# Gaps between on-chip tiles, and two pools swapped, in a one-core hybrid encoder layer

## The chip, the core and the metric

The kernel runs on one core of a Trainium2 chip, as one program. The metric is the device time of one execution in microseconds (us). The core has a matrix engine (TensorE, PE in the profile, whose weight loads have a row of their own, PEld), three engines for elementwise work (VectorE or DVE, ScalarE or ACT, GpSimd or POOL), and a queue on SyncE (SP) that issues most DMAs. Tiles lie in on-chip memory of 128 partitions; a tile's address is a byte offset that is the same in every partition.

## The reference, cut to what matters

```python
proj = x @ w_in                                  # 2048 tokens, 1024 -> 1312 columns
q  = rms(c_q) @ w_q_b;  kv = rms(c_kv) @ w_kv_b  # 8 heads, 64 + 32 rotary, values 64
o_mla = softmax(q @ k.T * 96**-0.5) @ v          # dense, 8 heads, all 2048 keys
o_swa = banded_softmax(q_s, k_s, sinks) @ v_s    # |t - s| <= 128, 8 heads, 2 key heads
x = layer_norm(alpha * x + concat(o_mla, o_swa) @ w_o)
h = conv3(x @ w_up) + conv_b;  g, u = split(h)   # 2 x 2816 columns
x = layer_norm(alpha * x + (gelu(g) * u) @ w_down)
```

## The kernel before

Every product is made of float32 values that are split into a high and a low part, both in the matrix engine's float32r type. `PASSES = ((0, 0), (0, 1), (1, 0))` are the three matmuls that one step of a product takes: high by high, high by low, low by high. A matmul names two on-chip operands: `lhsT`, the weights (128 columns, 512 bytes of each partition), and `rhs`, which is streamed (at most 512 columns, 2,048 bytes of each partition). Each matmul is preceded by its own weight load.

The five stages follow each other, and in each the matmuls stand in an order written out by hand:

1. **Projection and window attention** (lines 494 to 880). Per 128 tokens: three column groups of `w_in` (L598: weights `xT`, streamed `wi`; 16 tiles x 24 matmuls of 512 columns for each of two groups, and of 288 columns for the third), the low-rank products (L372: weights `cT`, streamed `wq` in 384 columns and `wkv` in 512; 192 each), window scores (L754: weights `q2`, streamed `kT`, 256 matmuls, 224 of them with 384 columns) and window values (L798: weights `vS`, streamed `pT`, 184 matmuls).
2. **Dense attention** (`Mla`, 8 heads x 16 query blocks, 128 periods). Per period 12 score matmuls (L205: weights `qT`, 96 rows, streamed `kT`), 16 transposes of the probabilities (L157: the data as weights, `ident` streamed, 128 columns), 8 value matmuls (L175: weights `v2`, streamed `pt`).
3. **Output projection** (`out_proj`, 16 tiles x 48 matmuls, L981: weights `mh`, for the first tile `m0`; streamed `wo`), layer norm, transposes and the sums that a Strassen-like scheme of 7 products takes, stored to `yS`.
4. **Up-projection** (`up_products`, 3,696 matmuls, L1382). Weights: five buffers `u0` to `u4`, used in turn, 12 matmuls each. Streamed: the 14 operand tiles `y00` to `y61` in pools `y_a` and `y_b`.
5. **Down-projection** (`down_products`, L1402). Seven stretches i = 0 to 6 of 264 matmuls. Weights: `a0`, `a1`. Streamed: in the odd stretches tiles `B` of pool `d_b`; in the even ones eleven tiles in places that the stage before has left: `r00` to `r11` and `T0`, `u0` to `u2`, and `T1`, `u3`, `u4`.

Pools are stacks: the left ones grow up from the constants, the right ones grow down from byte 229,344. A tile is rounded up to 32 bytes, and nothing else is aligned. 229,344 is 480 past a multiple of 512, and the right-hand tiles that are operands are whole multiples of 512 bytes, so they lie 480 past such a multiple. On the left the offset depends on the small tiles that stand below.

A tile may take a place that an earlier tile had; its first writer then waits for the last reader of the earlier one. One such place matters here. In `ffn`, pool `y_b` takes the place of `out_proj`'s pools: tile `y30` (101,152 to 109,344) has the place of `g1` and `b1`, the norm's gain and bias. It is written by `split_op(0, 3)` (L1098 and L1099) in step t = 0 of `up_products`; in step 1 follows, on the same ScalarE queue, the copy `s1` of the first product (L1246), which the third product (L1382, X) waits for. `b1` is read last by the POOL addition of the last tile's norm (L919). `y[ts]` is stored at L1017 on SP's queue, and on the same queue the next operand pieces are loaded (L1089) when `split_op` has read the ones before.

Of the kernel before, what the change touches and what calls it, by code (L numbers as in the profile page):

```python
# [12 lines left out]
F32 = mybir.dt.float32  # L13
# [8 lines left out]
P = 128  # L22
# [320 lines left out]
class Kern:  # L343
# [23 lines left out]
    def mm3(self, out, n, lhs, rhs):  # L367

        nc = self.nc
        for k in range(n):  # L370
            for i, (l, r) in enumerate(PASSES):
                nc.tensor.matmul(out, lhsT=lhs(k, l), rhs=rhs(k, r),  # L372
                                 start=(k == 0 and i == 0), stop=(k == n - 1 and i == 2))

    def consts(self, pool):
        nc = self.nc
        self.ident = pool.tile([P, P], F32, name="ident")
        make_identity(nc, self.ident)
        self.cw = pool.tile([P, 4, 2 * NF], F32, name="cw")
        one = pool.tile([P, 1], F32, name="one")  # L380
        nc.gpsimd.memset(one, 1.0)
        nc.scalar.copy(one, one)
        self.mhalf = pool.tile([P, 1], F32, name="mhalf")
        nc.gpsimd.memset(self.mhalf, -0.5)

    def warm_up(self, ps):

        t = ps.tile([P, 512], F32, name="M")
        for i in range(16):
            self.nc.tensor.transpose(out=t[:, i % 4 * P:(i % 4 + 1) * P], in_=self.ident, identity=self.ident)  # L390
# [103 lines left out]
    def project(self, mla, keep, heads_pool):  # L494
        nc, tc, a = self.nc, self.tc, self.a
        wide = ExitStack()
        with ExitStack() as st:
            pool = self.pools(st)
            wip = self.pools(wide)("p1wi", 1, side="right")
            cst = pool("p1c", 1)  # L500
# [10 lines left out]
            wsrc = w_in.rearrange("(k p) c -> p k c", p=P)  # L511
            wq = [cst.tile([P, 2, H * DQ], F32R, name=f"wq{i}") for i in range(2)]
            wkv = [cst.tile([P, 2, H * 128], F32R, name=f"wkv{i}") for i in range(2)]
            gcol = cst.tile([P, 4], F32, name="gcol")
            sink = cst.tile([P, SH], F32, name="sink")
            sink8 = cst.tile([P, SH], F32, name="sink8")
# [28 lines left out]
            sm = pool("p1s", 2)  # L545
# [36 lines left out]

            kT = [cst.tile([P, SKV, 6, P], F32R, name=f"kT{i}") for i in range(2)]
            nc.gpsimd.memset(kT[1].bitcast(F32), 0.0)

            qTs, vSs = {}, {}
# [82 lines left out]
            def latents_t(n):  # L671
                cn = cns.pop(n)
                t = psT.tile([P, 512], F32, name="T")
                for j in range(4):
                    nc.tensor.transpose(out=t[:, j * P:(j + 1) * P], in_=cn[:, j * P:(j + 1) * P], identity=self.ident)
                cT = cTs[n] = [sm.tile([P, 4, P], F32R, name=f"cT{i}", bufs=1) for i in range(2)]
                o = [v.rearrange("p k t -> p (k t)") for v in cT]
                nc.scalar.copy(o[0], t)
                nc.vector.tensor_sub(o[1], t, o[0].bitcast(F32))
# [61 lines left out]
            def window_p(n, g, d):  # L741

                lo, hi = span(n)
                assert hi - 1 in vSs
                nb = hi - lo
                nk = nb * P
                q2 = qTs[n]
                sl = slice(lo % 4, lo % 4 + nb)
                s = st8[n, g] = big.tile([P, 4, 384], F32, name="s", bufs=2)
                mx = sm.tile([P, 4], F32, name="mx")  # L750
                for j in range(4):
                    sp = psS.tile([P, 512], F32, name="Sp")
                    for i in range(2):
                        nc.tensor.matmul(sp[:, 0:nk], lhsT=q2[:, g * 4 + j], rhs=kT[i][:, g, sl], start=(i == 0), stop=(i == 1))  # L754
                    slope = 2.0 ** (-(g * 4 + j + 1))
                    nc.vector.scalar_tensor_tensor(s[:, j, 0:nk], d, -8.0 * slope, sp[:, 0:nk], op0=ALU.mult, op1=ALU.add)
                    if j % 2:
                        nc.vector.reduce_max(mx[:, j - 1:j + 1], s[:, j - 1:j + 1, 0:nk], axis=AX.X)
                    if j == 1:
                        yield  # L760
                hs = slice(g * 4, g * 4 + 4)
                nm = sm.tile([P, 4], F32, name="nm")
                nc.vector.tensor_max(nm, mx, sink8[:, hs])
                nc.vector.tensor_scalar(nm, nm, -0.125, 1.0, op0=ALU.mult, op1=ALU.mult)
                es = sm.tile([P, 4], F32, name="es")
                nc.vector.tensor_add(es, sink[:, hs], nm)
                sums = sm.tile([P, 4], F32, name="sums")
                for j in range(4):
                    nc.scalar.activation(s[:, j, 0:nk], s[:, j, 0:nk], AF.Exp, bias=nm[:, j:j + 1], scale=0.125,
                                         accum_out=sums[:, j:j + 1])  # L770
                nc.scalar.activation(es, es, AF.Exp)
                nc.vector.tensor_add(sums, sums, es)
                rec = sm.tile([P, 4], F32, name="rec")
                nc.vector.reciprocal(rec, sums)
                for j in range(4):
                    nc.gpsimd.tensor_scalar(s[:, j, 0:nk], s[:, j, 0:nk], rec[:, j:j + 1], 1.0, op0=ALU.mult, op1=ALU.mult)
# [41 lines left out]
            def do(token, n):  # L818
# [6 lines left out]
                elif name in ("x0", "x1"):  # L825
                    if m + 2 < NT and (name, m) not in gens:
                        gens[name, m] = x_parts(m + 2, int(name[1]))
                elif m < 0 or m >= NT:
                    return
                elif name in ("fk", "fq", "lt", "ds"):  # L830
                    if (name, m) not in gens:
                        gens[name, m] = {"fk": front_k, "fq": front_q, "lt": latents_t, "ds": distances}[name](m)
                elif name in ("k0", "k1", "k2", "k3"):
                    c = int(name[1])
                    mla.prep_k(0, c, psT)
                    mla.prep_v(0, c)
                    if c < 2:
                        mla.load_kv(0, c + 2)
                elif name == "q0":
                    mla.prep_q(0, 0, psT)  # L840
                elif name == "cl":
                    wide.close()
                    mla.open_heads(keep, heads_pool)
                    for c in range(2):
                        mla.load_kv(0, c)
                        mla.load_q(0, c)
                else:
                    if (name, m) not in gens:
                        gens[name, m] = (window_p(m, int(name[1]), gens["ds", m]) if name[0] == "p" else
                                         {"la": latents, "sq": swa_q, "sk": swa_kv, "hd": heads, "wo": window_o}[name](m))  # L850
                    if next(gens[name, m], gens) is gens:
                        done.add((name, m))
# [85 lines left out]
    def out_proj(self):  # L938
        nc, tc, a, wo = self.nc, self.tc, self.a, self.wo
        with ExitStack() as stack:  # L940
# [2 lines left out]
            self.op = [self.pools(self.opsA)("y_a", 1)]  # L943
            self.ops = [None] * 7
            pool = self.pools(stack)
            cst = pool("o_c", 1)
            sm = pool("o_s", 3)
            mp = pool("o_m", 2)
            yp = pool("o_y", 1)
            psT = pool("oT", 4, space=PSUM)  # L950
            psM = pool("oM", 4, space=PSUM)
# [113 lines left out]
    def open_weights(self):  # L1065

        w = self.wst = self.top("w_st", 1)
        self.FS = [f for i in range(NP) for f in (i, i + NP)] * 2
        self.prods = {7 * n + o: (n, s) for n in range(2 * NF) for s, o in enumerate(self.OFF)}
        self.rank = {t: i for i, t in enumerate(sorted(self.prods))}  # L1070
        self.r = [[w.tile([P, 2, 512], F32, name=f"r{q}{m}") for m in range(2)] for q in range(2)]
        self.u = [w.tile([P, 2, 512], F32R, name=f"u{i}") for i in range(3)]
        self.Tt = [w.tile([P, 2, 512], F32, name="T0")]
        self.hb = w.tile([P, 2, NF], F32, name="hb")

    def more_weights(self, pool):
        self.up = pool
        self.u += [pool.tile([P, 2, 512], F32R, name=f"u{i}") for i in range(3, self.UNITS)]
        self.Tt += [pool.tile([P, 2, 512], F32, name="T1"), pool.tile([P, 512], F32, name="T2")]
# [507 lines left out]
```

## Time and profile before

| | |
|---|---|
| median of 3 runs | 2936.74 us (2935.35 to 2937.01) |
| the profiled execution's own time | 2936.55 us |
| its span, first to last instruction | 2934.8 us |
| TensorE busy | 97% of the span, 13,943 matmuls |
| VectorE, ScalarE, GpSimd busy | 72%, 52%, 35% |
| mean granted TensorE clock | 0.988 of 2.4 GHz |

A matmul's shown duration includes a pipeline that the next matmul overlaps. The pace of matmuls is therefore read from the timeline, which merges neighbours of one kind into a row: the start of the next row less the start of this one, by the count of this one. A row of matmuls that follows a row of transposes also carries the end of the last transpose.

### The profile page before, as it was taken

How to read it: one execution, taken by the hardware profiler on the slowest of the kernel's cores; microseconds unless marked ns; L12 is line 12 of the kernel's file. 1: busy time of each engine (PE TensorE's matmuls, PEld its weight loads, DVE VectorE, ACT ScalarE, POOL GpSimd, SP SyncE). 2: the span in 40 equal slices, each digit the busy share in tenths (PEclk: the TensorE clock that was granted, in tenths of full speed). 3: DMA queues.
4: the chain of work that ended last, by engine and by line, in shares of the span. 5: the costliest groups of instructions: out<-in, count | busy, mean ns of one | idle time of the engine just before them, and what ended most of it. 6: DMA issues, size and time to landing. Idle time of an engine off the chain costs nothing.

```text
span 2934.8 us, 39778 instructions
## 1 busy us (share of the span) xinstructions
PE 2845.6 (97%) x13943; PEld 2345.6 (80%) x13943; DVE 2123.5 (72%) x3393; ACT 1527.5 (52%) x2830; POOL 1038.5 (35%) x1349
## 2 busy tenths in 40 slices
PE   8999998899999999999998999999999998999997
PEld 7888886688888888887787888887888887888875
DVE  6666676677777777777666888889877777666576
ACT  5555554667767776776233544445544444332332
POOL 4334343588888888887323000000000000000112
PEclk9999999899999999999999999999999999999999
DMA  4222222111101110111776645557545445955453
GB/s 155 82 71 81 72 58 68 37 33 33 31 24 33 33 31 24 33 31 48 215 241 216 190 147 152 158 161 231 153 140 148 142 138 189 340 198 178 159 178 114
DMA packets 353565, 349.95 MB, mean 119 GB/s; under 512 B 35184, under 2 KB 284372, under 8 KB 353364
## 3 DMA queue, kind: packets, MB, share of 16 engines
q1 hardware_dynamic: 350396, 337.80, 37.1%
q10 hardware_dynamic: 2968, 9.60, 1.0%
q8 instruction: 110, 1.80, 0.2%
q14 instruction: 91, 0.75, 0.1%
HBM read 223.06 MB, written 120.08 MB: 117 GB/s over the span
## 4 chain that ended last, share of the span: by engine, by line
PE 81%; DVE 7%; POOL 4%; DMA 3%; issue 3%; ACT 3%; SPq 0%; POOLq 0%; DVEq 0%; ACTq 0%
PE X L1382 12%; PE Sp L205 12%; PE D L1402 11%; PE W L1382 8%; PE O L175 8%; PE T L157 8%; PE M L598 5%; PE Y L1382 4%; PE Z L1382 4%; PE M L981 3%; DMA pw<-prow 2%; PE M L372 2%; PE M L798 1%; PE Sp L754 1%; PE T L787 1%
## 5 line engine op out<-in xcount | busy, mean ns | idle before, releaser
L205 PE MATMUL Sp<-kT,qT 96*128 96x512 f32 x1536 | 388.3, 402 | 5.9 <-ACT p L215 3.1
L1382 PE MATMUL X<-y,u 128*128 128x512 f32 x1584 | 385.1, 396 | 7.9 <-ACT s L1246 7.9
L207 DVE TENSOR_REDUCE mx<-Sp 128x1 f32<-128x1024 f32 x256 | 313.1, 1224 | 90.2 <-PE Sp L205 76.0
L1382 PEld LDWEIGHTS X<-y,u 128*128 128x128 f32 x1584 | 299.3, 189 | 78.2 <-ACT s L1246 8.3
L243 POOL TENSOR_SCALAR p<-p,rec 128x1024 f32<-128x1024 f32 x255 | 284.4, 1126 | 141.2 <-ACT stg L111 89.7
L205 PEld LDWEIGHTS Sp<-kT,qT 96*128 96x128 f32 x1536 | 281.0, 190 | 62.5 <-ACT p L215 4.9
L1455 POOL TENSOR_TENSOR patch<-hb 128x11 f32<-128x11 f32 x4 | 2.9, 735 | 874.6 <-ACT hb L1267 874.6
L215 ACT ACTIVATE p<-Sp,nm 128x1024 f32<-128x1024 f32 x256 | 287.7, 1124 | 5.4 <-DVE nm L209 5.3
L157 PE MATMUL T<-ident,p 128*128 128x128 f32 x2048 | 278.0, 276 | 5.8 <-POOL p L243 2.3
L157 PEld LDWEIGHTS T<-ident,p 128*128 128x128 f32 x2048 | 236.8, 141 | 56.4 <-POOL p L243 23.2
L224 ACT CAST pt<-T 128x512 fp32r<-128x512 f32 x256 | 137.8, 589 | 258.2 <-PE T L157 258.2
L598 PE MATMUL M<-wi,xT 128*128 128x512 f32 (+1 forms) x1152 | 267.4, 368 | 4.0 <-ACT wi L519 2.5
L175 PE MATMUL O<-pt,v 128*128 128x512 f32 x1024 | 271.2, 407 | 0.0
L1382 PE MATMUL W<-y,u 128*128 128x512 f32 x1056 | 259.6, 395 | 2.8 <-DVE hr L1287 2.8
L1382 PEld LDWEIGHTS W<-y,u 128*128 128x128 f32 x1056 | 198.4, 188 | 50.1 <-ACT hr L1251 2.1
L598 PEld LDWEIGHTS M<-wi,xT 128*128 128x128 f32 x1152 | 200.5, 190 | 36.0 <-ACT wi L519 2.9
L175 PEld LDWEIGHTS O<-pt,v 128*128 128x128 f32 x1024 | 183.4, 189 | 35.7 <-DVE pt L228 0.9
L1402 PE MATMUL D<-B,a 128*128 128x512 f32 x792 | 183.8, 394 | 4.9 <-DVE a L1443 4.9
L1402 PEld LDWEIGHTS D<-B,a 128*128 128x128 f32 x792 | 150.5, 190 | 37.7 <-DVE a L1443 6.1
L113 POOL TENSOR_TENSOR pt<-stg,pt 128x512 fp32r<-128x512 f32 x128 | 165.7, 1295 | 10.7
L228 DVE TENSOR_TENSOR pt<-T,pt 128x512 fp32r<-128x512 f32 x256 | 163.9, 681 | 2.7 <-ACT pt L224 2.5
L355 POOL TENSOR_TENSOR n2y<-n2ve,mhalf 128x1 f32<-128x1 f32 x16 | 26.6, 1663 | 393.2 <-DVE n2ve L1485 388.2
(317 smaller groups left out, 5553.5 us busy)
## 6 DMA issues: line engine op xcount, KB each, us to landing
r<-in_w_up SPq DMA_DIRECT2D x154, 256.0 KB, 3.6
araw<-hS SPq DMA_DIRECT2D x55, 704.0 KB, 4.2
oy<-in_w_down SPq DMA_DIRECT2D x132, 256.0 KB, 4.7
hS<-gs SPq DMA_DIRECT2D x110, 256.0 KB, 2.4
tS<-T SPq DMA_DIRECT2D x88, 256.0 KB, 2.2
T<-tS SPq DMA_DIRECT2D x88, 256.0 KB, 2.9
qkv<-nat SPq DMA_DIRECT2D x32, 512.0 KB, 5.4
oy<-yS SPq DMA_DIRECT2D x28, 512.0 KB, 5.8
```

The source lines that it names most:

```text
L113: nc.gpsimd.tensor_tensor(dst[1], sv, dst[0].bitcast(F32), op=ALU.subtract)
L157: nc.tensor.transpose(out=t[:, i * P:(i + 1) * P], in_=p[g // 2][:, k0:k0 + P], identity=self.k.ident)
L175: nc.tensor.matmul(ov, lhsT=vb, rhs=pt[w][:, i], start=(g == 0 and i == 0 and w == 0), stop=(g == 3 and i == 3 and w == 1))
L205: nc.tensor.matmul(sp[:, cc * 512:(cc + 1) * 512], lhsT=q[l], rhs=self.kTs[h][r][:, k0:k0 + 512], start=(i == 0), stop=(i == 2))
L207: nc.vector.reduce_max(mx[:, hf:hf + 1], sp, axis=AX.X)
L215: nc.scalar.activation(p[hf], sps[hf], AF.Exp, bias=nm, scale=self.scale, accum_out=sums[:, hf:hf + 1])
L224: nc.scalar.copy(o[g][0], self.k4(ts[g]))
L228: nc.vector.tensor_sub(o[g][1], self.k4(ts[g]), o[g][0].bitcast(F32))
L243: eng.tensor_scalar(p[hf], p[hf], rec, 1.0, op0=ALU.mult, op1=ALU.mult)
L598: nc.tensor.matmul(ov, lhsT=h[l][:, k % 4], rhs=wi[g][r][:, k], start=(k == 0 and i == 0), stop=(k == KD - 1 and i == 2))
L1382: nc.tensor.matmul(bk[n, bank], lhsT=w[:, l, k * P:(k + 1) * P], rhs=o[r][:, k], start=bool(new) and k == 0 and i == 0, stop=k == KH - 1 a ...
L1402: self.nc.tensor.matmul(d, lhsT=a[l][:, k], rhs=self.Bs[i, k][:, r], start=(k == 0 and x == 0), stop=(k == NP - 1 and x == 2))
```

## The change

Eight tiles are allocated that nothing reads or writes ("gaps"), and in `out_proj` the pool `o_m` (the tiles `mh`) is opened ahead of the pools `o_c` (`g1`, `b1`) and `o_s` (small tiles of the norm). No instruction is added, removed or reordered.

```diff
+    @staticmethod
+    def gap(pool, n, name="gap"):
+        pool.tile([P, n // 4], F32, name=name, bufs=1)
...
         nc.gpsimd.memset(self.mhalf, -0.5)
+        self.gap(pool, 96)
...
             wkv = [cst.tile([P, 2, H * 128], F32R, name=f"wkv{i}") for i in range(2)]
+            self.gap(cst, 384, "gap2")
...
+            self.gap(cst, 32)
             kT = [cst.tile([P, SKV, 6, P], F32R, name=f"kT{i}") for i in range(2)]
+            self.gap(cst, 384, "gap3")
...
+                if n == 0:
+                    self.gap(sm, 192)
                 cT = cTs[n] = [sm.tile([P, 4, P], F32R, name=f"cT{i}", bufs=1) for i in range(2)]
...
+                if n == 0 and g == 0:
+                    self.gap(sm, 448, "gap2")
                 rec = sm.tile([P, 4], F32, name="rec")
...
+            mp = pool("o_m", 2)
             cst = pool("o_c", 1)
             sm = pool("o_s", 3)
-            mp = pool("o_m", 2)
...
         self.hb = w.tile([P, 2, NF], F32, name="hb")
+        self.gap(w, 96)
```

What it does to the places, worked out from the tiles' order and sizes (bytes past a multiple of 512; w is the weights' operand, s the streamed one):

| matmuls | before | after |
|---|---|---|
| L598 | w 96, s 480 | w 480, s 480 |
| L372 | w 416, s 384 | w 480, s 480 |
| L754 | w 96, s 480 | w 480, s 480 |
| L798 | w 416, s 480 | w 480, s 480 |
| L205 | w 480, s 480 | the same |
| L175 | w 480, s 384 | w 480, s 480 |
| L981, tiles 1 to 15 | w 448, s 480 | w 480, s 480 |
| L981, tile 0 | w 480, s 480 | the same |
| L1382, u0 to u2 | w 384, s 288 | w 480, s 480 |
| L1382, u3 and u4 | w 480, s 288 | w 480, s 480 |
| L1402, odd stretches | w 288, s 288 | w 480, s 480 |
| L1402, even: r, T0, u0 to u2 | w 288, s 384 | w 480, s 480 |
| L1402, even: T1, u3, u4 | w 288, s 480 | w 480, s 480 |
| transposes | w as the data lies, s 128 | s 128; the data mostly at 480 |

In `out_proj` the `mh` tiles now lie at 101,344 to 117,728, `g1` and `b1` at 117,728 to 125,920. `y30` and `y31` (101,344 to 117,728) so take the place of `mh`, and `y40` and `y41` (117,728 to 134,112) that of `g1`, `b1`, the norm's small tiles and the first of its `yt`.

## Rows read from the trace of the kernel before

**Rows 1.** Busy time of each engine by stage: window, length, engines (instructions), clock, DMA.
```profile
0.00:520.00 520.00, 486.38 (x2630) 417.22 (x2631) 353.37 (x811) 280.95 (x734) 206.69 (x480) 0.99 0.29 86
520.00:1400.00 880.00, 867.97 (x4871) 723.02 (x4870) 635.82 (x1038) 606.79 (x1131) 718.00 (x729) 0.99 0.12 33
1400.00:1600.00 200.00, 197.74 (x901) 160.22 (x900) 129.63 (x238) 60.19 (x76) 61.41 (x41) 0.99 0.71 220
1600.00:2470.00 870.00, 859.33 (x3697) 695.31 (x3696) 701.35 (x918) 442.88 (x742) 4.68 (x3) 0.99 0.53 162
2470.00:2934.80 464.80, 434.21 (x1852) 349.80 (x1850) 303.36 (x391) 136.72 (x148) 47.70 (x98) 0.97 0.57 198
```

**Rows 2.** Timeline of TensorE, up-projection, 1905 to 1922 us: start, length, instruction, count.
```profile
1907.34 2.97 PE L1382 MATMUL W<-y,u 128*128 128x512 f32 x12
1910.15 2.91 PE L1382 MATMUL Z<-y,u 128*128 128x512 f32 x12
1912.90 5.72 PE L1382 MATMUL X<-y,u 128*128 128x512 f32 x24
1918.46 2.97 PE L1382 MATMUL W<-y,u 128*128 128x512 f32 x12
```

**Rows 3.** Timeline of TensorE, down-projection, first rows of stretches 1, 2 and 3.
```profile
2540.93 60.03 PE L1402 MATMUL D<-B,a 128*128 128x512 f32 x264
2600.80 1.57 PE L1402 MATMUL D<-r,a 128*128 128x512 f32 x6
...
2662.30 2.00 PE L1402 MATMUL D<-B,a 128*128 128x512 f32 x8
```

**Rows 4.** Timeline of TensorE, dense attention, one period and a little more.
```profile
903.60 1.48 PE L157 MATMUL T<-ident,p 128*128 128x128 f32 x12
904.83 2.11 PE L175 MATMUL O<-pt,v 128*128 128x512 f32 x8
906.78 0.60 PE L157 MATMUL T<-ident,p 128*128 128x128 f32 x4
907.14 2.99 PE L205 MATMUL Sp<-kT,qT 96*128 96x512 f32 x12
909.97 1.74 PE L157 MATMUL T<-ident,p 128*128 128x128 f32 x12
```

**Rows 5.** Timeline of TensorE, projection, and below it output projection.
```profile
303.31 3.03 PE L598 MATMUL M<-wi,xT 128*128 128x512 f32 x12
306.18 0.87 PE L754 MATMUL Sp<-kT,q 128*128 128x384 f32 x4
...
1481.56 2.96 PE L981 MATMUL M<-kT,mh 128*128 128x512 f32 x12
1484.36 0.86 PE L981 MATMUL M<-v,mh 128*128 128x512 f32 x3
```

**Rows 6.** Timeline of all engines where the up-projection begins; in brackets the idle time before.
```profile
1601.72 1.24 ACT L915 ACTIVATE oy<-oy,n1nb,n1y 128x1024 f32<-128x1024 f32 x1
1605.46 2.34 POOL L919 TENSOR_TENSOR oy<-oy,b 128x1024 f32<-128x1024 f32 x1
1607.82 0.34 SPq L1017 DMA_DIRECT2D y<-oy  x1
1607.83 1.99 ACT L1098 CAST y<-oy 128x1024 fp32r<-128x1024 f32 x2 [4.87 <-POOL oy L919]
1610.16 1.45 SPq L1089 DMA_DIRECT2D oy<-yS  x2
1610.36 2.08 PE L1382 MATMUL X<-y,u 128*128 128x512 f32 x4 [7.88 <-ACT s L1246]
```

**Rows 7.** Groups of GpSimd instructions by line and shape: count, busy us, mean ns, idle before.
```profile
L113 POOL TENSOR_TENSOR pt<-stg,pt 128x512 fp32r<-128x512 f32 x128 | 165.7, 1295 | 10.7
L113 POOL TENSOR_TENSOR qT<-stg,qT 96x512 fp32r<-96x512 f32 x31 | 39.7, 1282 | 2.6
```

## The prediction

> **What bounds the kernel now.** I read the busy time by stage first [rows 1]. In every stage TensorE is the busiest engine: 868 of 880 us in the dense attention, 859 of 870 in the up-projection, 198 of 200 in the output projection, and there the clock is granted at 0.99. The next engine is far behind: VectorE 701 of 870 in the up-projection, GpSimd 718 of 880 in the attention. Only the first stage (486 of 520) and the last (434 of 465) hold waits that add up. So what a matmul costs is what the kernel costs, and the reader should next look at the pace of matmuls, by start times in the timeline.
>
> There the same matmul (128 rows, 512 columns, same split types) has several paces. In the down-projection one line runs a stretch over the tiles `B` and then a stretch over other places. 264 matmuls over `B` take 2600.80 - 2540.93 = 59.87 us, 226.8 ns each; the next 264 take 2662.30 - 2600.80 = 61.50 us, 233.0 ns each [rows 3]. Weights and instructions are alike; what differs is where the streamed tile lies: `B` is as far from a multiple of 512 bytes as the weights (288 and 288), the others are not (384 or 480 against 288). In the up-projection twelve matmuls take 1910.15 - 1907.34 = 2.81 us with `u2` (234.2 ns) and 1912.90 - 1910.15 = 2.75 us with `u3` (229.2 ns); the 24 over `u4` and `u0` take 5.56 us, one of either kind [rows 2]. The streamed tile lies at 288; `u0` to `u2` lie at 384, `u3` and `u4` at 480.
>
> Behind transposes a row needs a correction: 12 transposes take 904.83 - 903.60 = 1.23 us and 4 take 907.14 - 906.78 = 0.36, so one is worth 0.109 us and some 0.08 us of the last falls to the row behind. The 8 value matmuls then take (906.78 - 904.83 - 0.08) / 8 = 233.8 ns and the 12 score matmuls (909.97 - 907.14 - 0.08) / 12 = 229.2 ns [rows 4]. Scores have both operands at 480, values one at 480 and one at 384. L598 (96 against 480) has (2.87 - 0.08) / 12 = 232.5 ns, L981 (448 against 480) 2.80 / 12 = 233.3 ns [rows 5].
>
> So equal distance goes with 226.8 to 229.2 ns, unequal with 229.2 to 234.2.
>
> **The change part by part.** The gaps add no instruction; they move left tiles so that all operands of these matmuls lie at 480, beside right ones that stay there. What each class will then cost no row shows exactly (480 and 480 with 128 rows is rare before), so I bound it: below by `B`'s 226.8 ns, above by the scores' 229.2. In both MLP stages I take 227, since `B`'s matmuls are of the same shape and stage; in the attention the scores' 229.2, since the same engines run beside them; in projection and output projection 228, between.
>
> Up-projection: three of five buffers, 2,218 matmuls, gain 234.2 - 227 = 7.2 ns, 16.0 us; the other 1,478 gain 2.2 ns, 3.3 us. Of 19.3 I count 95%, 18.3 us, since VectorE has slack [rows 1].
>
> Down-projection: the four even stretches, 1,056 matmuls, gain 6.0 ns. Stretches 2 and 4 in full, 3.2 us; 0 and 6 stand at the stage's ends, where its waits must lie, so half, 1.6. Together 4.8 us. `B` loses nothing at 227.
>
> Dense attention: 1,024 value matmuls gain 4.6 ns, 4.7 us; scores and transposes keep their operands' distance or their pace.
>
> Output projection: 15 tiles of 48, 720 matmuls, gain 5.3 ns, 3.8 us.
>
> Projection: 768 matmuls of L598 gain 4.5 ns, 3.5 us. The rest I scale from it by columns: 384 with 288 columns at 2.5 ns, 416 with 384 at 3.4, 376 with 512 at 4.5, together 4.1 us. The stage waits for 7% of its time, so I count three quarters of 7.6, 5.7 us.
>
> The swapped pools change one wait. As the up-projection begins, ScalarE's write of `y30` (L1098) starts at 1607.83 after 4.87 us of idling until the norm's last addition (L919, 1605.46 plus 2.34) has read `b1`, whose place `y30` takes. Queued behind it is the copy `s1` (L1246), and TensorE idles 7.88 us for that, until 1610.36 [rows 6]. After the change `y30` takes the place of `mh`, which matmuls alone read, and these are over before the up-projection's first. The write can then follow ScalarE's previous instruction, which ends at 1602.96: 4.87 us earlier. What is late next is the load of the following operand pieces. It is issued at 1610.16, after `split_op` has read the pieces before, but on SP's queue the store of the last tile (1607.82, again behind L919) stands ahead of it [rows 6], so it can move to about 1608.2, 2 to 3 us, and `y40` itself now waits for `b1`, which is free by then. I take 4.0 us, between 3 and 4.87. If some other release holds `y30`, it is 0.
>
> The other engines' operands move by the same bytes. GpSimd's subtraction takes 1295 ns into a tile at 384 and 1282 into one at 480 [rows 7]: no cost at 480. The gaps cost space only. Their cover is that later stages' tiles still take the places of tiles long done; where one does not, the price is one wait, of the size of the 4.87 us above.
>
> One rule speaks against all of this. The rows show a pace that goes with the place of two operands that different reads fetch: 226.8 against 233.0 ns on one line [rows 3]. The Trainium skill (SBUF — State Buffer, "Who interferes with whom") says that TensorE has two independent read ports, one for the streamed operand and one for weights, and that it never waits on anyone. By that rule the place could not matter and the gaps would give 0 us; by the rows they give 37. The trace disagrees with the rule as far as these rows go.
>
> Sum: 18.3 + 4.8 + 4.7 + 3.8 + 5.7 + 4.0 = 41.3 us, of the profiled execution's 2936.55 us: 2895.3, so 2895 us. That execution stands 0.2 us below the median of the runs.
>
> **The rivals.** Partial: the equal distance helps only where one matmul class is long alone, and in mixed stages the time comes back as waits. Then only `u0` to `u2` gain, at the scores' floor: 2,218 x 5.0 = 11.1 us, and the swap's 4.0: 2921 us. For it speak the waits in the first and last stages; against it, that TensorE is busy 98% and more in the three middle ones [rows 1].
>
> No effect: the distance is not the cause, but something else that goes with these tiles, such as which engine wrote them last or the side they lie on. Then the swap alone is left, 2932.6 us, 0.14% and within what counts as the same (a measurement of this kernel tells about 0.2% from no change). For it: each class is one set of tiles. Against: on L1402 the tiles differ in nothing else, and pace follows distance on six lines.
>
> Slower: the pace depends on where each operand lies and not on their distance, and 480 for both is a bad place for 128 rows. The worst pace in the rows is 234.2 ns; at that, `u3` and `u4` lose 5.0 x 1,478 = 7.4 us, `B` 7.4 x 792 = 5.9, the even stretches 1.2 x 1,056 = 1.3, the other classes some 3.0 (1,024 x 0.4, 720 x 0.9, 768 x 1.7, rounded up for the rest), 17.6 in all, and with the swap's 4.0 the kernel ends at 2950 us. The mean pace over the seven classes counted above is 232.1 ns for 8,056 matmuls, and the swap is worth another 0.5 ns of each: from 232.6 ns at 480 and 480 on the kernel is slower. For it: `u3` and `u4` gain with 480 against 288 too, so distance is not all. Against: the scores run at 229.2 with both at 480 [rows 4].
>
> **How the numbers follow.** Forecast 0.76, partial 0.10, no effect 0.08, slower 0.06. Lowest time: 226.8 ns everywhere and nothing hidden, 16.4 + 3.5 (up) + 6.5 (down) + 7.2 (attention) + 4.7 (output) + 9.6 (projection) + 4.9 (swap) = 52.8 us, 2884. Highest time of the forecast: 229.2 everywhere, 11.1 (up), nearly 0 (down: 2.0 in stretches 2 and 4, less 1.9 lost on `B`), 3.8, 3.0 and 2.7, and no swap: 20.7 us, 2916. Two us below and one above for runs among themselves: 2882 to 2917. It leaves out all three rivals and little else. Faster by over 0.2% are forecast and partial, 0.86; the same 0.08; slower 0.06.
>
> **What would show it.** Right: 24 matmuls of the up-projection in 5.45 us whichever buffers; 264 in about 60.0 us in the even and odd stretches of the down-projection alike; 8 value matmuls in 1.91 to 1.92 us; the third product of the up-projection after 3 to 4 us of idling in place of 7.88, with no wait for L919 ahead of L1098. Wrong: paces of 232 ns and more left with both operands at 480, or shorter rows with longer waits between them, or a transpose slower than 0.109 us because its data have moved; a longer wait where a stage begins would speak for a tile that took the place of a live one.

## The result and the profile after

| | before | after |
|---|---|---|
| median | 2936.05 us (2934.86 to 2937.01, 4 runs) | 2903.67 us (2903.20 to 2904.40, 4 runs) |
| profiled execution | 2936.55 us, span 2934.8 | 2904.40 us, span 2902.6 |
| mean granted clock | 0.988 | 0.987 |

The ratio is 0.989, with a 95% interval of 0.9873 to 0.9907: 1.1% faster, where 2895 us (0.986) was forecast. Line numbers have moved in the kernel after: L598 is now L608, L754 L766, L919 L933, L981 L995, L1017 L1031, L1089 L1104, L1098 and L1099 L1113 and L1114, L1246 L1261, L1382 L1397, L1402 L1417.

The windows of the kernel after, one for each stage and cut at the first matmul of the stage (the up-projection's first 76 rows of TensorE, 68 products and 8 transposes, where the swap acts, by themselves). Columns: window, length, busy time of TensorE, weight loads, VectorE, ScalarE and GpSimd (instructions), clock, DMA share, GB/s.

```profile
2.69:526.22 523.53, 491.91 (x2659) 422.79 (x2659) 361.07 (x821) 283.83 (x740) 206.63 (x476) 0.98 0.30 86
526.22:1395.71 869.49, 858.19 (x4844) 718.66 (x4845) 630.62 (x1028) 603.11 (x1124) 715.13 (x724) 0.99 0.12 32
1395.71:1587.25 191.54, 189.14 (x882) 156.64 (x880) 123.36 (x232) 58.48 (x75) 56.01 (x34) 0.99 0.74 229
1587.25:1615.05 27.80, 20.32 (x80) 15.62 (x78) 17.76 (x19) 12.99 (x22) 9.36 (x9) 0.88 0.70 221
1615.05:2442.99 827.94, 824.13 (x3637) 681.58 (x3636) 691.50 (x905) 431.02 (x723) 0.00 (x0) 1.00 0.54 162
2442.99:2902.60 459.61, 427.33 (x1849) 348.92 (x1847) 302.67 (x391) 136.34 (x147) 47.51 (x98) 0.97 0.58 200
```

The same windows of the kernel before are 525.07, 873.41, 195.45, 27.46, 846.51 and 464.21 us long, so the stages answer to the terms of the sum as follows:

| stage | forecast | measured |
|---|---|---|
| projection | -5.7 | -1.5 |
| dense attention | -4.7 | -3.9 |
| output projection | -3.8 | -3.9 |
| start of the up-projection (swap) | -4.0 | +0.3 |
| rest of the up-projection | -18.3 | -18.6 |
| down-projection and end | -4.8 | -4.6 |
| sum | -41.3 | -32.2 |

Four stages stand within 0.8 us of the forecast; the projection and the swap miss by 8.5 together. Each side is one profiled execution. The projection of e3 below, whose places are those of before, takes 523.26 us, as little as after (523.53), so the 1.5 us are not clear of what runs differ by; the start of the up-projection takes 28.51 us in e11, the changed kernel again, so the swap shows no gain in either. First the terms that came true. TensorE's timeline after, in the up-projection (answers to [rows 2]) and, below, the first rows of the down-projection's stretches 2 and 3 (to [rows 3]):

```profile
1910.61 2.88 PE L1397 MATMUL W<-y,u 128*128 128x512 f32 x12
1913.33 2.88 PE L1397 MATMUL Z<-y,u 128*128 128x512 f32 x12
1916.05 5.60 PE L1397 MATMUL X<-y,u 128*128 128x512 f32 x24
1921.49 0.84 PE L1397 MATMUL W<-y,u 128*128 128x512 f32 x3
...
2572.16 2.20 PE L1417 MATMUL D<-r,a 128*128 128x512 f32 x9
...
2632.00 2.20 PE L1417 MATMUL D<-B,a 128*128 128x512 f32 x9
```

Every twelve take 2.72 us now, 226.7 ns each, whichever `u` they read; the 24 take 5.44. The even stretch takes 2632.00 - 2572.16 = 59.84 us, as long as the odd one before (59.87); before it took 61.50.

The short rows are another matter. TensorE's timeline after in the projection, with rows like those of [rows 5]:

```profile
301.49 3.01 PE L608 MATMUL M<-wi,xT 128*128 128x512 f32 x12
304.34 0.87 PE L766 MATMUL Sp<-kT,q 128*128 128x384 f32 x4
...
306.10 0.86 PE L608 MATMUL M<-wi,xT 128*128 128x512 f32 x3
306.80 0.87 PE L766 MATMUL Sp<-kT,q 128*128 128x384 f32 x4
```

Both operands of L608 lie at 480 here, yet the three matmuls take 306.80 - 306.10 = 0.70 us, 233 ns each, and the twelve behind the transposes 304.34 - 301.49 = 2.85 us, against 2.87 before. The stage's groups by line agree: L608's 768 matmuls are busy for 208.0 us after and 208.9 before, where a gain of 3.5 us was forecast; in e3, at the old places, they are busy for 208.7.

In the dense attention (answers to [rows 4]) the values lie between:

```profile
908.31 2.08 PE L175 MATMUL O<-pt,v 128*128 128x512 f32 x8
910.23 0.60 PE L157 MATMUL T<-ident,p 128*128 128x128 f32 x4
910.59 3.01 PE L205 MATMUL Sp<-kT,qT 96*128 96x512 f32 x12
913.44 1.48 PE L157 MATMUL T<-ident,p 128*128 128x128 f32 x12
```

With 0.08 us off for the transpose ahead, the eight values take 230.0 ns each in this period, which is among the fastest: over the 125 rows of eight in the trace the median is 1.935 us, 231.9 ns each (1.952 us and 234.0 ns before, 229.2 ns forecast). The scores, whose operands did not move, take (2.85 - 0.08) / 12 = 230.8 here; their median is 2.836 us (2.833 before). What the stage gained stands in its groups, busy time first, before and then after:

```profile
L157 PE MATMUL T<-ident,p 128*128 128x128 f32 x2048 | 278.0, 276 | 5.8 <-POOL p L243 2.3
L175 PE MATMUL O<-pt,v 128*128 128x512 f32 x1024 | 271.2, 407 | 0.0
...
L157 PE MATMUL T<-ident,p 128*128 128x128 f32 x2048 | 275.4, 275 | 5.9 <-POOL p L243 2.2
L175 PE MATMUL O<-pt,v 128*128 128x512 f32 x1024 | 269.6, 406 | 0.0
```

The values gained 1.6 us, the transposes 2.6.

Last, all engines where the up-projection begins (answers to [rows 6]):

```profile
1593.97 1.98 ACT L1113 CAST y<-oy 128x1024 fp32r<-128x1024 f32 x2
1594.14 2.35 POOL L931 TENSOR_TENSOR oy<-oy,g 128x1024 f32<-128x1024 f32 x1 [3.04 <-ACT oy L929]
1595.03 5.86 DVE L1114 TENSOR_TENSOR y<-oy,y 128x1024 fp32r<-128x1024 f32 x2 [3.01 <-ACT y L1113]
1596.47 4.61 PE L1397 MATMUL X<-y,u 128*128 128x512 f32 x12 [3.49 <-ACT s L1261]
1596.57 3.24 POOL L933 TENSOR_TENSOR oy<-oy,b 128x1024 f32<-128x1024 f32 x1
1599.83 0.34 SPq L1031 DMA_DIRECT2D y<-oy  x1
1600.27 8.90 SPq L1104 DMA_DIRECT2D oy<-yS  x4
1605.35 2.22 ACT L1113 CAST y<-oy 128x1024 fp32r<-128x1024 f32 x2 [7.36 <-DMA oy<-yS]
1608.10 2.50 PE L1397 MATMUL X<-y,u 128*128 128x512 f32 x5 [3.98 <-ACT U L1261]
```

The write of `y30` (the first row) no longer idles, and starts before L933 does. TensorE idles 3.49 us ahead of the third product, in place of 7.88. But a new wait of 3.98 us stands ahead of the fifth (the last row): ScalarE idled 7.36 us for a load that was issued at 1600.27. That load stands behind the store of the last tile (1599.83), and the store behind L933, which now runs 3.24 us (2.34 before) beside VectorE's subtractions (5.86 us for two, 2.36 before). ScalarE's two writes need a load each. The second is issued when VectorE's second subtraction has read its piece (1600.89):

```profile
1600.91 0.51 SPq L1104 DMA_DIRECT2D oy<-yS  x1
```

### The profile page after: what moved, and what is told of

Read it like the earlier page. It is cut to its first block, busy times and chain, and to the rows that moved or that the text cites. A ratio compares the mean times of both kernels' runs of the same rounds, so it can differ in the third digit from the quotient of the medians.

```text
span 2902.6 us, 39779 instructions
## 1 busy us (share of the span) xinstructions
PE 2811.0 (97%) x13943; PEld 2344.2 (81%) x13943; DVE 2127.0 (73%) x3393; ACT 1527.2 (53%) x2830; POOL 1036.8 (36%) x1349
## 4 chain that ended last, share of the span: by engine, by line
PE 78%; DVE 8%; issue 4%; DMA 4%; POOL 4%; ACT 3%; SPq 0%; POOLq 0%; DVEq 0%; ACTq 0%
PE Sp L205 12%; PE X L1397 11%; PE D L1417 10%; PE O L175 8%; PE T L157 8%; PE W L1397 8%; PE M L608 6%; PE Y L1397 4%; PE Z L1397 4%; PE M L372 2%; PE M L812 1%; PE Sp L766 1%; POOL yt L931 1%; PE T L801 1%; PE T L119 1%
## 5 line engine op out<-in xcount | busy, mean ns | idle before, releaser
L205 PE MATMUL Sp<-kT,qT 96*128 96x512 f32 x1536 | 388.5, 402 | 6.2 <-ACT p L215 3.1
L1397 PE MATMUL X<-y,u 128*128 128x512 f32 x1584 | 377.2, 392 | 7.5 <-ACT U L1261 4.0
L1397 PEld LDWEIGHTS X<-y,u 128*128 128x128 f32 x1584 | 299.0, 189 | 70.5 <-ACT U L1261 4.4
L205 PEld LDWEIGHTS Sp<-kT,qT 96*128 96x128 f32 x1536 | 281.0, 190 | 62.9 <-ACT p L215 4.8
L157 PE MATMUL T<-ident,p 128*128 128x128 f32 x2048 | 275.4, 275 | 5.9 <-POOL p L243 2.2
L157 PEld LDWEIGHTS T<-ident,p 128*128 128x128 f32 x2048 | 236.5, 141 | 53.4 <-POOL p L243 19.3
L608 PE MATMUL M<-wi,xT 128*128 128x512 f32 (+1 forms) x1152 | 266.5, 368 | 4.4 <-DVE wi L528 2.2
L175 PE MATMUL O<-pt,v 128*128 128x512 f32 x1024 | 269.6, 406 | 0.0
L1397 PE MATMUL W<-y,u 128*128 128x512 f32 x1056 | 254.0, 389 | 3.8 <-DVE hr L1302 3.8
L1397 PEld LDWEIGHTS W<-y,u 128*128 128x128 f32 x1056 | 198.0, 188 | 46.1 <-DVE hr L1302 2.9
L608 PEld LDWEIGHTS M<-wi,xT 128*128 128x128 f32 x1152 | 200.1, 190 | 35.6 <-DVE wi L528 3.0
L175 PEld LDWEIGHTS O<-pt,v 128*128 128x128 f32 x1024 | 183.1, 189 | 35.1 <-DVE pt L228 0.9
L1417 PE MATMUL D<-B,a 128*128 128x512 f32 x792 | 183.7, 394 | 4.9 <-DVE a L1458 4.9
L1417 PEld LDWEIGHTS D<-B,a 128*128 128x128 f32 x792 | 150.5, 190 | 37.6 <-DVE a L1458 6.1
```

Of the source, the lines that this page charges most:

```text
L157: nc.tensor.transpose(out=t[:, i * P:(i + 1) * P], in_=p[g // 2][:, k0:k0 + P], identity=self.k.ident)
L175: nc.tensor.matmul(ov, lhsT=vb, rhs=pt[w][:, i], start=(g == 0 and i == 0 and w == 0), stop=(g == 3 and i == 3 and w == 1))
L205: nc.tensor.matmul(sp[:, cc * 512:(cc + 1) * 512], lhsT=q[l], rhs=self.kTs[h][r][:, k0:k0 + 512], start=(i == 0), stop=(i == 2))
L608: nc.tensor.matmul(ov, lhsT=h[l][:, k % 4], rhs=wi[g][r][:, k], start=(k == 0 and i == 0), stop=(k == KD - 1 and i == 2))
L1397: nc.tensor.matmul(bk[n, bank], lhsT=w[:, l, k * P:(k + 1) * P], rhs=o[r][:, k], start=bool(new) and k == 0 and i == 0, stop=k == KH - 1 a ...
L1417: self.nc.tensor.matmul(d, lhsT=a[l][:, k], rhs=self.Bs[i, k][:, r], start=(k == 0 and x == 0), stop=(k == NP - 1 and x == 2))
```

## The experiments

Three theories were open. *Distance*: equal distance makes the pace, wherever both operands lie. *Settling*: after transposes, or on another interruption, the next matmuls go at an uneven pace until they fall into step, so short rows gain little. *Late load*: at the start of the up-projection one wait has only made room for the next. Each diff is against the kernel after, but for e3.

**e1, the gaps without the swap.**

```diff
-            mp = pool("o_m", 2)
             cst = pool("o_c", 1)
             sm = pool("o_s", 3)
+            mp = pool("o_m", 2)
```

> All eight gaps, pools in the old order: the tiles mh lie 128 past a multiple of 512, the streamed wo at 480, and y30 takes the place of g1 and b1 again. Theory A (the swap takes the norm's addition out of ScalarE's way, but the load of the next operand pieces, behind the last tile's store on SP's queue, ends as late as before): the first 76 matmuls of the up-projection take 27.5 to 28.5 us, as with the swap (27.80) and before (27.46); the output projection goes back to 233 ns a matmul and 195.4 us; in all 2907 to 2908 us. Theory B (the swap is worth the predicted 4 us at the start of the up-projection): the first 76 take 31 to 32 us, in all 2911 to 2912.

(The gaps are seven by the diff, not eight.) Measured: 2910.76 us, ratio 0.9911 (0.9896 to 0.9926). The output projection takes 195.60 us, as before the change (195.45), the up-projection's first 76 rows 28.68, its rest 829.04: theory A, though the whole lies 3 us above its range. The timeline of this kernel, output projection and start of the up-projection:

```profile
1476.82 2.96 PE L995 MATMUL M<-kT,mh 128*128 128x512 f32 x12
1479.62 0.86 PE L995 MATMUL M<-v,mh 128*128 128x512 f32 x3
...
1605.05 1.99 ACT L1113 CAST y<-oy 128x1024 fp32r<-128x1024 f32 x2 [4.87 <-POOL oy L933]
1607.58 4.50 PE L1397 MATMUL X<-y,u 128*128 128x512 f32 x12 [9.97 <-ACT s L1261]
```

With `mh` back at 128 the twelve take 2.80 us again (233.3 ns), and the wait for L933 is back. The stretch is only 0.9 us longer than in the kernel after, and 0.2 longer than in e11: the swap pays by the 4.1 us of distance in the output projection, and hardly by the wait.

**e2, all operands at multiples of 512**, by other gaps, one of them at the right end (and two in place of three buffers for the norm's small tiles, for room).

```diff
-        self.gap(pool, 96)
+        self.gap(pool, 128)
-            sm = pool("o_s", 3)
+            sm = pool("o_s", 2)
+            self.gap(pool("rgap", 1, side="right"), 480)
```

> Left and right operands all at exact multiples of 512 bytes (a gap of 480 at the right end, 128 in place of 96 among the constants; the norm's small tiles of the output projection get 2 buffers for 3, to fit). Distance theory: equal distance is all that counts, so the paces are those of the changed kernel, 227 ns in the up-projection, 2902 to 2906 us. Place theory: where an operand starts counts too, so that operands that start on a multiple cross fewer of them: the pace in long rows moves by 3 ns or more either way, and the time by 20 us or more.

Measured: 2902.77 us, 0.9885 (0.9869 to 0.9902); projection 522.34 us, attention 867.01, output projection 191.50, first 76 rows 28.90. Its up-projection:

```profile
1913.46 5.60 PE L1397 MATMUL X<-y,u 128*128 128x512 f32 x24
1918.90 1.29 PE L1397 MATMUL W<-y,u 128*128 128x512 f32 x5
```

The 24 take 5.44 us, 226.7 ns each, as in the kernel after: 0 and 0 is as good as 480 and 480. The place does not matter there, the distance does.

**e3, the kernel before with one gap, behind `hb`.** The up-projection's streamed tiles move to 384, the place of `u0` to `u2`.

```diff
         self.hb = w.tile([P, 2, NF], F32, name="hb")
+        w.tile([P, 24], F32, name="gap", bufs=1)
```

> The kernel before with the last gap alone, 96 bytes behind hb: the up-projection's streamed tiles move from 288 to 384, u0 to u2 stay at 384 (now equal), u3 and u4 at 480 (distance now as in the value matmuls of before, streamed 384 and weights 480); in the down-projection a and B are both at 384, r, T0, u0 to u2 at 384 as well, T1, u3 and u4 at 480. Distance theory: u0 to u2 go to 227 ns, u3 and u4 from 229 to 233 or 234; 264 matmuls of an even stretch take 60.3 us (three of eleven tiles stay at 233); in all about 2924 us. Place theory (480 is a good place for the weights, or for both): u3 and u4 stay at 229 and u0 to u2 at 234, in all 2930 us or more.

Measured: 2925.99 us, 0.9965 (0.9952 to 0.9978). Its up-projection:

```profile
1916.97 2.88 PE L1383 MATMUL Y<-y,u 128*128 128x512 f32 x12
1919.70 2.97 PE L1383 MATMUL X<-y,u 128*128 128x512 f32 x12
1922.50 2.97 PE L1383 MATMUL W<-y,u 128*128 128x512 f32 x12
1925.31 2.91 PE L1383 MATMUL Z<-y,u 128*128 128x512 f32 x12
```

Three buffers in five take 2.72 us, the other two 2.80 and 2.81: 226.9 and 233.8 ns. `u3` and `u4` have become slower (2.75 before) though they did not move; the streamed tiles are now 96 ahead of them in place of 192. So the same two places change rank with the distance alone.

One expectation was missed: an even stretch of the down-projection took 60.85 us (2591.58 to 2652.43), not 60.3. Tiles at both distances take turns there, and the trace, start to start, shows what that costs: behind the last matmul over a tile at the unequal distance, those over equal ones take 232, 233, 236, 224, 231, 236, 228, 233 and 231 ns, and only the tenth is at 227. No transpose stands near. This is settling.

**e4, settling in the attention: values right behind the scores** (with 7 buffers of `pt`; the swap stayed in, other than expected below), so that transposes stand ahead of the scores only.

```diff
+        if av:
+            self.values(*av)
         if prev:
             (ph, pb), pv = prev
...
         if av:
-            self.values(*av)
```

> The changed kernel without the pool swap, and in the dense attention the 8 value matmuls follow the 12 scores directly, ahead of the 12 transposes (a period later than before, with a seventh pair of pt buffers). Settling theory (after transposes the pace needs some nine matmuls to settle, whatever the distance; only then equal distance gives 227 ns): the 8 value matmuls, now the 13th to 20th after transposes, take 1.82 us, 227 ns each. Traffic theory (in the attention the other engines' accesses hold the pace up): they stay at 231 to 232 ns, 1.85 to 1.86 us without what a row behind transposes carries. The whole is expected to be slower under either, by some tens of us, since the fourth group of transposes then waits for a buffer.

Measured: 3042.72 us in its one run. The order brings waits of its own: TensorE waits each period for VectorE's copies of `pt` (0.5 us) and in the midst of the scores. The values took 1.85 us for eight (231 ns), the figure of the traffic theory; but by the settling theory the wait inside the scores' row starts the pace over, so that the same figure can follow from it. The test decided nothing.

**e5, no transposes between values and scores.** It leaves out the fourth group of transposes; the values take the third group in its place.

```diff
-            t3 = self.pt_tr(ph, pb, pv, 3)
+            t3 = ts[2]
```

> The changed kernel without the fourth group of 4 transposes in each period of the dense attention (the third group's result is used in its place, so the attention's result is not the reference's); the copies behind it stay. In half of the periods the 12 scores then follow the 8 values with no transposes between. Settling theory (after transposes equal distance needs some nine matmuls to come to 227 ns): these 12 scores, 9th to 20th after transposes, take 2.72 to 2.73 us, 227 ns each; the values in front of them stay at 231 to 232 ns. Traffic theory (the other engines' accesses hold the attention's pace up): the scores stay at 229 ns, 2.75 us. If waits come up between the rows the pace starts over, and only rows without a wait are read.

Measured: 2880.03 us in its one run (four transposes less in each of 128 periods). TensorE's timeline, and below it the end of the same rows in a narrower window:

```profile
1002.06 2.11 PE L175 MATMUL O<-pt,v 128*128 128x512 f32 x8
1004.01 2.88 PE L205 MATMUL Sp<-kT,qT 96*128 96x512 f32 x12
...
1005.83 1.07 PE L205 MATMUL Sp<-kT,qT 96*128 96x512 f32 x4
```

The first eight scores take 1005.83 - 1004.01 = 1.82 us, 227.5 ns each; the values, still behind transposes here, take (1.95 - 0.08) / 8 = 233.8. (The last score waits for its buffer, so the whole row is no measure.) This row is one of the better half. Of the 66 rows of scores behind values, 32 take 1.82 or 1.83 us for the first eight and are at 227 ns from the second to the fourth matmul on; 28 take 1.84 and are uneven for five matmuls (232, 236, 228, 233 and 231 ns) before they are at 227. In the kernel after, behind transposes, the scores are uneven for nine (median 228 to 236 ns, one of 224). With operands at the same places the pace depends on what stands ahead of the row, as settling has it, though in half of the rows a shorter settling is left.

**e6, without the scaling of the probabilities**, to see if GpSimd's traffic holds up the short rows.

```diff
-            for hf in range(2):
-                eng = nc.vector if hf == 0 and cur == (H - 1, NT - 1) else nc.gpsimd
-                eng.tensor_scalar(p[hf], p[hf], rec, 1.0, op0=ALU.mult, op1=ALU.mult)
```

> The changed kernel without the scaling of the probabilities by 1 / sum in the dense attention (L243, 284 us of GpSimd), so the attention's result is not the reference's. Traffic theory: with GpSimd's largest work gone the 12 scores, beside which it mostly runs, fall from 229 towards 227 ns (row 2.85 to 2.82 us behind transposes). Settling theory: rows as before, scores 2.83 to 2.86 us, values 1.92 to 1.94 us, and the time of the attention hardly moves.

Measured: 2897.93 us in its one run. The short rows are unchanged: over all rows of the trace the median is 1.936 us for eight values and 2.858 for twelve scores, against 1.935 and 2.836 in the kernel after. This theory fell. But the attention did move, by 9.2 us (860.34 against 869.49): TensorE's transposes, which wait for the scaled probabilities, are busy for 265.8 us in place of 275.4.

**e7, the last store on GpSimd's queue**, so that the late load need not follow it on SP's.

```diff
-                nc.sync.dma_start(out=self.y[ts, :], in_=r)
+                (nc.gpsimd if i == NT - 1 else nc.sync).dma_start(out=self.y[ts, :], in_=r)
```

> The changed kernel with the store of the last tile of the output projection (L1017 of before) issued from GpSimd's queue, so that SP's queue does not wait for the norm's last addition ahead of the loads of the next operand pieces. Queue theory (that store holds the loads): the first load is issued about 2.5 us earlier, when VectorE has read the first half, and the idling of 3.98 us ahead of the fifth product shrinks to 1 or 2 us. Port theory (the loads wait for VectorE, whose subtraction runs beside GpSimd's addition at 2.5 and 3.4 us in place of 1.2): the second pair of loads is issued as late as before and the idling stays above 3 us. In all between 2901 and 2904 us.

Measured: 2905.84 us, 0.9901 (0.9884 to 0.9917). Start of its up-projection:

```profile
1598.25 11.75 SPq L1104 DMA_DIRECT2D oy<-yS  x4
1608.93 5.34 PE L1397 MATMUL X<-y,u 128*128 128x512 f32 x12 [4.28 <-ACT U L1261]
```

The first load is issued 1.9 us earlier (11.1 us behind the stage's first matmul at 1587.17, not 13.0), and ScalarE's write for it starts 1.6 us earlier (1603.69, 16.5 us behind it, not 18.1). Yet the idle time ahead of the fifth product is 4.28 us, not less, because the second load is later:

```profile
1601.47 0.34 SPq L1104 DMA_DIRECT2D oy<-yS  x1
```

That is 14.3 us behind the first matmul, not 13.7: it waits for VectorE's second subtraction, as the port theory said. So the queue held the first load, and not the one that the product waited for.

**e8, e2 with e7's store.**

> All operands at exact multiples of 512, as in the second run, and the last store from GpSimd's queue. In long rows 227 ns as in both; in the dense attention the faster settling at 0 (some four matmuls in place of nine) is worth 2 to 3 us, in the projection 1; in all 2899 to 2902 us if it repeats, 2903 to 2904 if the attention's gain at 0 was chance.

Measured: 2902.21 us (2898.72 to 2902.53), 0.9888 (0.9874 to 0.9903), attention 866.73: e2 again, between the two ranges expected.

**e9, the norm's last addition on VectorE**, so that GpSimd does not add beside the subtractions.

```diff
-                for _ in self.norm(sm, st, r, g1, b1, "n1", *((0, True) if i >= NT - 2 else ())):
+                for _ in self.norm(sm, st, r, g1, b1, "n1", *((0 if i == NT - 2 else D, True) if i >= NT - 2 else ())):
```

> The changed kernel with the last tile's addition of b1 (L919 of before) on VectorE instead of GpSimd. Port theory (VectorE's two subtractions for y31 and y30 are held by GpSimd's addition beside them): they take 1.2 us each in place of 2.5 and 3.4, the second pair of operand pieces is loaded 0.5 to 1 us earlier relative to the first product, and the idling ahead of the fifth product falls below 3.5 us. Against it: the subtractions stay above 2 us. The whole moves by less than can be measured, 2901 to 2905 us.

Measured: 2905.00 us, 0.9891 (0.9876 to 0.9906). Start of its up-projection:

```profile
1594.48 2.35 DVE L1114 TENSOR_TENSOR y<-oy,y 128x1024 fp32r<-128x1024 f32 x2
1595.73 9.83 SPq L1104 DMA_DIRECT2D oy<-yS  x4
1604.49 4.38 PE L1397 MATMUL X<-y,u 128*128 128x512 f32 x12 [3.88 <-ACT U L1261]
```

The two subtractions take 2.35 us in place of 5.86, so the neighbour was what slowed them. The first load is issued 11.8 us behind the first matmul (1583.95), the second 12.9 behind it (1596.86; 13.7 in the kernel after). But ScalarE's writes start only 0.3 us earlier for it (17.8 and 19.0 us behind the first matmul, not 18.1 and 19.3), and the idle time is still 3.88 us, where the port theory expected less than 3.5.

**e10 and e11, the end.** e10 is e2 with e9's addition, e11 the changed kernel again, on the same chip.

> All operands at exact multiples of 512, and the last addition on VectorE. Attention 866 to 868 us from the first score to the first matmul of the output projection (869.5 with all at 480), projection 522 to 523 us (523.5); in all 2899 to 2903 us, 1 to 4 below the changed kernel on the same chip.

> The changed kernel once more, to stand beside the run before on the same chip: 2902 to 2905 us, attention 869 to 870 us, projection 523 to 524.5 us.

Measured: e10 2904.24 us, 0.9889 (0.9874 to 0.9904); e11 2904.76 us, 0.9891 (0.9876 to 0.9906). e10 was expected 1 to 4 us below e11 and is not. Whether the place is worth anything in the attention is open: it takes 867.0, 866.7 and 867.9 us with all at 0, and with all at 480 it takes 869.5 and 869.1 (the changed kernel), 869.3 (e1) and 869.6 (e7), but 866.2 in e9. No version beats the changed kernel by more than the runs differ.

## Why the prediction was right, and where its sum was not

**The cause and the long rows: right.** That equal distance sets the pace is shown by e2 (another place, the same pace) and e3 (the same places of `u3` and `u4`, another distance, another pace); the rivals that said "no effect" and "a bad place" fell with the result itself. The partial one (2921 us) fell with the 12 us that even stretches, output projection and attention gained together; right in it is that a stage of short, mixed rows gains little, but by pace and not by waits. The 227 ns taken for both MLP stages measured 226.7, and the terms came out at 18.6 for 18.3 and 4.6 for 4.8. The output projection's 3.8 measured 3.9, and e1 took it away by putting `mh` back. The rule of the Trainium skill (SBUF — State Buffer, "Who interferes with whom"), by which TensorE never waits, would have left 0 us of these; the trace disagrees with it by 6 ns of 233 in each matmul.

**The projection: mis-sized, 5.7 forecast, 1.5 measured, and even that not clear of noise.** The step that failed: "Projection: 768 matmuls of L598 gain 4.5 ns". They gained 208.9 - 208.0 = 0.9 us, 1.2 ns each, and e3, without any change here, has 208.7 us and a stage as short as after. The step gave short rows the pace of long ones. In the output projection after one sees how a row gets there (timeline; the last row is a narrower window on the end of the second; eight transposes end just ahead of the first row):

```profile
1469.18 3.02 PE L995 MATMUL M<-kT,mh 128*128 128x512 f32 x12
1472.03 0.84 PE L995 MATMUL M<-v,mh 128*128 128x512 f32 x3
1472.71 2.20 PE L995 MATMUL M<-wo,mh 128*128 128x512 f32 x9
...
1470.66 1.53 PE L995 MATMUL M<-kT,mh 128*128 128x512 f32 x6
```

Behind the transposes the first six take 1470.66 - 1469.18 - 0.08 = 1.40 us (233 ns), the next six 1.37 (228), and those that follow 226.7 (0.68 for three). A tile of 48 matmuls settles and profits; the projection's rows of mostly 3 to 12 are over first. The trace after shows it there too, start to start: in the rows of nine that follow score matmuls of 384 columns, the matmuls take 230, 233, 235, 225, 231, 235, 228, 232 and 231 ns on average of 15 rows, and from the second on that is within 1 ns what the first nine behind transposes take in the output projection (behind the first one 233, 236, 224, 231, 236, 228, 233 and 231, average of 13 tiles). So a row of another shape interrupts as transposes do. e3 has the same nine in the down-projection, and e5 shows in the attention that the same scores settle sooner when no transposes stand ahead of them. e6 shows that GpSimd's scaling has no part in the pace. For the projection itself no run was made in which its rows were longer.

**The attention: the sum came near by luck, 4.7 forecast, 3.9 measured.** The step that failed: "1,024 value matmuls gain 4.6 ns, 4.7 us; scores and transposes keep their operands' distance or their pace." The values gained 1.6 us, a third of it; "the scores' 229.2" was the pace of a row of twelve that is not settled yet, and had been read as that of equal distance. The other 2.6 us came in the transposes, which the forecast put at nothing. It is no chance of one run: e3, with the attention's places of before, has 278.0 and 271.2 us again, e11 275.2 and 269.9. Back to back a transpose takes 109 ns before and after, so the gain lies in when they can start; what lets them start earlier no run shows.

**The swap: right up to the first wait, wrong in the sum, 4.0 forecast, -0.3 measured.** The write of `y30` moved ahead of L933, and the third product's wait fell to 3.49 us (3 to 4 were named). The step that failed: "it can move to about 1608.2, 2 to 3 us" for the load that is late next. Counted from the stage's first matmul (1596.62 before, 1587.25 after), it was issued 13.54 us behind it before and 13.02 after, and the time came back as 3.98 us ahead of the fifth product. Three parts of that are shown.

First, VectorE and GpSimd got into each other's way. The subtractions that free the pieces began 4.5 us earlier (7.78 us behind the first matmul, 12.28 before), which put them beside the norm's last multiplication and addition on GpSimd. They ended only 1.0 us earlier, and L933, ahead of the store, took 0.9 us longer. Second, the product waits for two loads. e7 moved the first alone; e9 moved the first by 1.2 us and the second by 0.8, and 0.3 was left of it when they landed. Third, the forecast has no term for TensorE's clock. TensorE idled 7.47 us in the two waits, 0.41 less than in the one before, and still the stretch became longer. Before, the granted clock fell once, in the long wait, to 0.50 of 2.4 GHz, the level of 1.2, and was back at 1.00 about when the third product was over. After, it fell once while the third product ran, rose, and fell again in the second wait, so that the fifth product began at 0.50:

```profile
1608.10:1611.00 2.90, 2.90 (x7) 2.32 (x8) 2.90 (x5) 0.99 (x2) 0.00 (x0) 0.50 0.65 199
```

In such a stretch a matmul starts 427 ns behind the one before. The first twelve of the fifth product take 4.25 us after (1608.10 to 1612.35) and 2.80 before (1618.54 to 1621.34); of these 1.45 us the third product gives back 0.83 (4.45 in place of 5.28).

Why the earlier loads of e9 land so little earlier is open. The windows speak for transfers ahead of them in the DMA engines: in the ten microseconds from 8.3 us behind the stage's first matmul these were busy for 0.95 of the time after, 0.81 before. First before, then after:

```profile
1605.00:1615.00 10.00, 4.64 (x11) 3.68 (x12) 3.57 (x4) 4.48 (x7) 2.71 (x2) 0.53 0.81 265
```

```profile
1595.50:1605.50 10.00, 7.64 (x24) 5.48 (x24) 6.59 (x4) 2.64 (x6) 4.23 (x2) 0.83 0.95 291
```

No run took such transfers away, so this is argued only.

**The range.** Its upper end counts 3.8 us for the attention at 229.2 ns, where the prediction's own term at that pace is 4.7; the end would lie 0.9 us lower, and the result is far from it. Of the signs named, 24 matmuls in 5.45 us, 264 in 60.0 and the third product's wait came; eight values in 1.91 to 1.92 us came in few rows.

## What to carry to other kernels

Where TensorE is the bound and one matmul shape shows several paces, put streamed operand and weights at equal distance from multiples of 512 bytes; it costs a few hundred bytes of gaps, and long unbroken rows gain up to 3%. Size the gain by row length: the pace to forecast for a short row is read from a short row whose operands already lie so, at the same position behind transposes, not from a long one. And before a removed wait is counted, follow every load that the next step needs to its landing, ask which engines the earlier work will now run beside, and see at what clock TensorE comes out of the waits that are left.

## What the runs showed of the hardware

- **The distance has a sign.** Streamed less weights, 128 rows and 512 columns, long rows: 0 gives 226.7 ns, -96 gives 233.8 to 234.2, -192 gives 229.2, +32, +96 and +192 give 233 (the last two in one mixed row of the down-projection). No long row has its operands 256 apart, so whether the measure is 512 bytes or 256 is open.
- **Settling.** With both operands at 480 the matmuls behind transposes go at 224 to 236 ns, by their position (means over thirteen tiles of the output projection), for nine matmuls, and only then at 226.7. The same sequence stands behind matmuls of another column count (projection) and behind matmuls at an unequal distance (e3). With all operands at 0 they are at 227 from the fourth on, and the first twelve take 2.82 us in place of 2.85 (e2: 1465.74 to 1468.56), so for this the place does count a little.
- **VectorE and GpSimd took turns.** A subtraction of 128x1024 float32 on VectorE takes 1.2 us alone, a multiplication or addition of that size on GpSimd 2.34. Side by side they show 2.5 and 3.4 us, and 2.35 and 3.24. But their ends are 1596.49 (L931), 1597.57 (first subtraction), 1599.81 (L933) and 1600.89 (second): each comes 1.08, 2.24 and 1.08 us behind the one ahead, about the time that the operation takes alone. So they look held one after the other rather than slowed together.
- **The clock.** At a granted clock of 0.50 a matmul of 512 columns takes 427 ns, at 1.00 it takes 227 to 234. It fell in a wait of 7.88 us, behind one of 3.49 and in one of 3.98.
